# A decoder layer with routed experts on one core: block lists of six fixed experts from ranks alone, the shift added as rows are turned, the left-over branch between blocks 25 and 26, final sums of two tiles on TensorE

## The chip, the cores and the metric

The kernel runs on one core of one Trainium2 chip. The metric is the device time of one execution in microseconds (us). The core has a matrix engine (TensorE, "PE" in the profile, its weight loads "PEld"), a vector engine (DVE), a scalar engine (ACT), GpSimd (POOL), and SyncE (SP), which here only issues DMA transfers. Each engine works through its own instructions in order and waits on semaphores for the others. Transfers issued by SP and ACT go through hardware queues, those with a list of row numbers (gathers and scatters) are issued by POOL.

## The reference

One step of a hybrid decoder layer for 512 prompt rows and 8 sample rows, all in float32. The first part (projection, sparse attention, a convolution branch, output projection, residual) is untouched by the change. What follows it matters here:

```python
# x: residual rows (512 prompt rows + 8 sample rows, D = 1024); mods: 6 adaLN vectors
h = rmsnorm(x, norm2_g) * (1.0 + mods[4]) + mods[3]     # scale, then shift
# group = top-1 of 4, experts = top-2 of its 8; w: their two weights
y = sum over the 2 chosen experts e of
        w_e * (silu(h @ w_gate[e]) * (h @ w_up[e])) @ w_down[e]   # 1024 -> 256 -> 1024
x = x + mods[5] * y
y_out = rmsnorm(x, final_g)
```

There are 32 experts. A row goes to two of them; the numbers are known only once the router has run.

## The kernel before

The rows of all experts are put in blocks of 64 places. There are 36 ordinary blocks: the six experts with fixed places (their 18 weight tensors of 1 MiB are fetched ahead of the routing, `fetch`) have blocks 0 to 5, the four fullest of the others two blocks each, the rest one. 16 more blocks take what is left over; they stand in a branch (`tc.If(nxv > 0)`) that isn't taken with these data.

**Routing.** For each tile of 128 rows `project` forms the residual `x1`, `rows` scales it by its inverse root (ACT), by `A2b` (POOL, L1280), adds the shift `B2b` (POOL, L1281) and writes the rows `h` to `hrow` in memory. `choose` picks the experts on DVE, `place` turns ranks into places. Once the last tile (3) is ranked, DVE forms the block lists: which row stands in each place (`gix`), where its result goes (`six`), its weight (`wtb`), and which expert follows which (`exi`, by which SP addresses the weights of blocks 6 and on).

**Expert stage.** A pair of blocks is handled together: `gather` (POOL, L1627) fetches the 128 rows of a pair from `hrow` by `gix`, `turned` transposes them on PE (L1640, eight 128x128 pieces in two halves) and copies the halves out, one on ACT and one on DVE. For each block `up` multiplies by gate and up weights (L1650, gate and up products side by side), `hidden` forms silu times up on ACT and DVE, `flip` transposes that (L1663), `down` multiplies by the third weight (L1672), DVE scales the result (`ot`, L1676) and POOL scatters it into `yrow` (L1677). `run` sets the order: the down product of a block comes after the up product of the next; gather(p+1) is issued when pair p is turned. The weights come through SP, three loads of 1 MiB per expert, into 21 pages that are handed out again in the order in which they come free; eight loads can be outstanding.

**Branch.** After block 35 each engine loads `nxi` and compares (L1730, L1731). On the path not taken POOL does one more step, an ISA instruction that the profile calls INC_SWDGE_SEM: it brings the counters of POOL's eight transfer queues to where the branch would have left them.

**Final stage.** The scattered results are loaded as four tiles (`yt`, two halves of 512 KB each), added to the residual on DVE (L1754, L1758), squared on ACT, rooted on POOL, scaled on DVE (L1777) and stored. The sample rows (`ysq`, `fs`) are summed on POOL (L1781 to L1783).

A scheduler orders instructions on each engine by the order of the code and by `issue_after`, which pins an instruction behind another.

Of the kernel before, what the change touches and what calls it, by code (L numbers as in the profile page):

```python
# [24 lines left out]
NF = 6  # L25
# [6 lines left out]
GT, TH, TF = (), (1, 1, 1, 2), (1, 1, 1, 2)  # L32
# [148 lines left out]
def body(tc, I, O, dbg=lambda *a: None):  # L181
# [658 lines left out]
    A2T, B2T = cp.tile([128, 8], F32, name="A2T"), small("B2T")  # L840
# [242 lines left out]
    x1s = cp.tile([128, 256], F32, name="x1s", tag="c2")  # L1083
    zs = e2.tile([128, 4, 32], F32, name="zs", bufs=1)
# [75 lines left out]
    BO = box(3, 10, NBLK, half_=True)  # L1160
    OH3 = BO.rearrange("p f a b -> p (f a b)")[:, :960].rearrange("p (a b c) -> p a b c", a=10, b=3)
# [17 lines left out]
    def choose(i):  # L1179
# [17 lines left out]
        V.tensor_tensor(Cb[:, i], OH[:, i, 0], OH[:, i, 1], op=ALU.add)  # L1197
        pps[i] = tps("pps", (128, 32))
# [4 lines left out]

    def place(i):
        m = eb
        V.tensor_tensor(m, OH[:, i], pps[i].unsqueeze(1).to_broadcast([128, 2, 32]), op=ALU.mult)
        r, k, r_ = rk[:, 0, 2 * i:2 * i + 2], kk[:, 2 * i:2 * i + 2], rk[:, 1, 2 * i:2 * i + 2]
        V.tensor_reduce(r, m, axis=AX.X, op=ALU.add)
# [3 lines left out]
        for j in range(2):  # L1212
# [6 lines left out]
                        s3.unsqueeze(3).to_broadcast([128, 2, 3, 32]), op=ALU.mult)  # L1219
        V.scalar_tensor_tensor(k, k, -1.0, s3[:, :, 2], op0=ALU.mult, op1=ALU.mult)  # L1220
        if i == 4:
            V.tensor_scalar(k, k, K("inv"), None, op0=ALU.add)

    def new_rows():
# [8 lines left out]
        V.tensor_tensor(h2s, h2s, m4[:, 3], op=ALU.add)  # L1233
        for q in range(4):
            S.dma_start(hrow[512:520, :].rearrange("b (c r j) -> b c r j", r=4, j=32)[:, :, q],
                        h2s[32 * q:32 * q + 8].rearrange("p (c j) -> p c j", c=8))
# [13 lines left out]
    def project(i, n):  # L1250
# [5 lines left out]
        V.scalar_tensor_tensor(xh, pA, ra[:, 0, i:i + 1], xh, op0=ALU.mult, op1=ALU.add)  # L1256
        SP.dma_start(xrow[128 * i:128 * i + 128, 512 * n:512 * n + 512], xh)
# [14 lines left out]
    def rows(i):  # L1272
# [12 lines left out]
        place(i)  # L1285
# [38 lines left out]
    later = []  # L1324
# [3 lines left out]
    def tile_start(i):  # L1328
# [15 lines left out]
        if i == WOI:  # L1344
            load_wo(0, 2)
            for v, r in ((A2b, 4), (B2b, 3)):
                SP.dma_start(v, mrow[r - 2:r - 1, :].to_broadcast([128, 1024]))
# [129 lines left out]
    fetch(PRE[2])  # L1477

    pct = tps("pct", (32, 1))
    pcb = acc("pcb", (128, 32))  # L1480
    for n, i in enumerate(order):
        PE.matmul(pct, Cb[:, i, :], onb[:, 0:1], start=(n == 0), stop=(n == 4))
    for n, i in enumerate(order):
        PE.matmul(pcb, onb, Cb[:, i, :], start=(n == 0), stop=(n == 4))
    hl = cp.tile([32, 12], BF16, name="hl")
    V.scalar_tensor_tensor(hl[:, 0:1], pct, 64.0, K("dmask")[:32], op0=ALU.is_gt, op1=ALU.mult)
    V.tensor_tensor(hl[:, 1:2], K("dmask")[:32], hl[:, 0:1], op=ALU.subtract)
    V.tensor_scalar(hl[:, 4:12], K("thr")[:32], pct, None, op0=ALU.is_lt)
    with nc.allow_low_precision(reason="a whole number up to 8"):
        V.tensor_reduce(hl[:, 2:3], hl[:, 4:12], axis=AX.X, op=ALU.add)  # L1490
    px = acc("px", (128, 3, 33))
    col = lambda k: hl[:, k:k + 1].to_broadcast([32, 128])
    PE.matmul(px[:, 0, :], col(0), K("su")[:32, :33], start=True, stop=True)
    PE.matmul(px[:, 1, :], col(1), K("su")[:32, :33], start=True, stop=False)
    PE.matmul(px[:, 1, :], col(0), K("al")[:32, :33], start=False, stop=True)
    PE.matmul(px[:, 2, :], col(2), K("su")[:32, :33], start=True, stop=True)

    T = cp.tile([128, 3, 32], BF16, name="T")
    hB = cp.tile([128, 32], F32, name="hB")
    q = cp.tile([128, 4, 33], F32, name="q")  # L1500
# [12 lines left out]
    with tc.issue_after(mark["V"].ins):
        V.tensor_copy(pos[:, P_], K("eio")[:, :NF])
# [304 lines left out]
```

## Time and profile before

| | us |
|---|---|
| three runs of the kernel before | 792.86, 795.72, 796.38 (median 795.72) |
| the profiled execution | 789.56 |
| its span, first to last instruction | 787.8 |
| mean granted TensorE clock, share of full speed | 0.944 |
| PE busy | 683.7 (87% of the span) |
| DVE busy | 440.4 (56%) |
| ACT, POOL busy | 213.7 (27%), 208.3 (26%) |

A timeline row of the profile gives the start, the duration, the engine, the line, the operation with output and inputs and their shape, the number of instructions, and in brackets how long the engine stood idle before it and for whom it waited. L1650 is line 1650 of the kernel before. "q" behind an engine's name marks what its sequencer does, such as issuing a transfer. A window row gives busy time and, in brackets, the number of instructions of each engine within a stretch, then the granted clock (1.00 is 2.4 GHz, 0.50 is 1.2 GHz), the share of time that the 16 DMA engines were busy, and what they moved.

### The profile page before, as it was taken

Reading aid. Unit: us, or ns where it says so; the run is one execution under the profiler, and the core shown is the slowest. Engines: PE = TensorE matmul, PEld = TensorE weight load, DVE = VectorE, ACT = ScalarE, POOL = GpSimd, SP = SyncE. Lnnn points to the kernel's source line nnn. Section 1 sums busy time; section 2 is a strip of 40 time slices with the busy share of each in tenths; the row PEclk is TensorE's granted clock in tenths of the full one; section 3 lists DMA queues with packets and bytes.
Section 4 is the critical chain, followed back from the end, with each engine's and each line's share of the span. In section 5 each row is a group of like instructions: output and inputs, shape, how many; then the busy total and the mean of one; then the engine's idle time right before and its main releaser. Section 6 shows DMA issues by size and latency. Waiting matters only on the chain. (4 is left out here: it accounts for less than half of the span.)

```text
span 787.8 us, 12614 instructions
## 1 busy us (share of the span) xinstructions
PE 683.7 (87%) x4888; PEld 414.4 (53%) x4888; DVE 440.4 (56%) x960; ACT 213.7 (27%) x491; POOL 208.3 (26%) x182
## 2 busy tenths in 40 slices
PE   4999888997999988999789998289999999999910
PEld 3655777775786446644435444155555555554400
DVE  2444729999985758723776745843333333333245
ACT  1255721121113457634245323010110101010001
POOL 5134305035030101135602303312222222221114
PEclk9999999998999999999979999589999999999965
DMA  9985425644799303700004666679999999999954
GB/s 340 420 324 203 160 81 215 244 161 192 266 343 407 136 2 131 285 0 1 1 16 165 248 251 240 257 248 418 420 406 350 410 418 418 417 419 420 370 177 176
DMA packets 42332, 200.02 MB, mean 254 GB/s; under 512 B 10733, under 2 KB 14205, under 8 KB 22677
## 3 DMA queue, kind: packets, MB, share of 16 engines
q1 hardware_dynamic: 29341, 156.27, 50.7%
q0 software_dynamic: 10336, 40.95, 13.5%
q10 hardware_dynamic: 2592, 1.95, 0.8%
q8 instruction: 40, 0.66, 0.3%
q14 instruction: 23, 0.19, 0.1%
HBM read 187.82 MB, written 22.15 MB: 267 GB/s over the span
## 5 line engine op out<-in xcount | busy, mean ns | idle before, releaser
L591 DVE SCALAR_TENSOR_TENSOR y<-u,c,y 128x511 f32<-128x511 f32 (+23 forms) x120 | 103.7, 896 | 2.1
L1655 ACT ACTIVATE hd<-pgu 64x256 f32<-64x256 f32 x36 | 13.5, 375 | 200.4 <-PE pgu L1650 200.4
L1677 POOL DMA_INDIRECT yrow<-ot,six x36 | 39.1, 1085 | 99.4 <-DVE ot L1676 87.9
L1650 PE MATMUL pgu<-eu,mB 128*64 128x256 f32 x256 | 61.7, 384 | 1.9 <-DMA eu<-in_WU 1.9
L1650 PE MATMUL pgu<-eg,mB 128*64 128x256 f32 x256 | 62.2, 384 | 0.0
L1672 PE MATMUL pd<-ed,hTe 128*64 128x512 f32 x240 | 57.3, 598 | 0.8 <-issue 0.8
L1650 PE MATMUL pgu<-eu,mA 128*64 128x256 f32 x224 | 54.0, 384 | 1.8 <-DMA eu<-in_WU 1.8
L1650 PE MATMUL pgu<-eg,mA 128*64 128x256 f32 x224 | 54.2, 384 | 0.0
L1676 DVE SCALAR_TENSOR_TENSOR ot<-pd,wtb,mt 128x512 f32<-128x512 f32 x36 | 27.0, 751 | 44.3 <-PE pd L1672 44.3
L1656 DVE TENSOR_TENSOR hd<-pgu,hd 64x256 f32<-64x256 f32 x36 | 15.4, 428 | 59.1 <-ACT hd L1655 59.1
L1650 PEld LDWEIGHTS pgu<-eg,mB 128*64 128x64 f32 x256 | 32.8, 136 | 19.9 <-issue 5.1
L1381 ACT ACTIVATE P<-pSp,ast 128x128 f32<-128x128 f32 (+3 forms) x64 | 33.2, 534 | 24.2 <-DVE ast L1376 23.9
L1376 DVE TENSOR_REDUCE ast<-pSp 128x1 f32<-128x384 f32 (+3 forms) x44 | 27.3, 632 | 21.7 <-PE pSp L1371 21.6
L1650 PEld LDWEIGHTS pgu<-eg,mA 128*64 128x64 f32 x224 | 28.9, 136 | 17.3 <-issue 4.6
L225 DVE COPY hTe<-hTp 128x128 f32<-128x128 f32 x36 | 10.5, 291 | 48.3 <-PE hTp L1663 48.3
L370 PE MATMUL pr<-cTs,wc 128*64 128x256 f32 x256 | 37.1, 400 | 0.0
L1253 PE MATMUL woA<-wo,qT 128*128 128x512 f32 x64 | 35.9, 681 | 0.2 <-DVE rt L1175 0.2
L1650 PEld LDWEIGHTS pgu<-eu,mB 128*64 128x64 f32 x256 | 33.0, 136 | 4.0 <-DMA eu<-in_WU 2.8
L361 PE MATMUL cT<-CI,cR 128*128 128x128 f32 x128 | 21.1, 302 | 10.9 <-DVE cR L386 10.7
L1650 PEld LDWEIGHTS pgu<-eu,mA 128*64 128x64 f32 x224 | 28.9, 136 | 2.9 <-DMA eu<-in_WU 2.3
L1109 PE MATMUL woC<-wo,y 128*128 128x512 f32 x64 | 30.2, 605 | 0.1
L1413 PE MATMUL oT<-P,kv 128*64 128x512 f32 x80 | 28.6, 614 | 0.0
(572 smaller groups left out, 1654.5 us busy)
## 6 DMA issues: line engine op xcount, KB each, us to landing
eg<-in_WG SPq DMA_DIRECT2D x26, 1024.0 KB
eu<-in_WU SPq DMA_DIRECT2D x26, 1024.0 KB
ed<-in_WD SPq DMA_DIRECT2D x26, 1024.0 KB
wada<-in_WA SPq DMA_DIRECT2D x16, 1024.0 KB
wada<-in_WA POOLq DMA_DIRECT2D x8, 1024.0 KB, 15.2
WG<-in_WG SPq DMA_DIRECT2D x6, 1024.0 KB
WU<-in_WU SPq DMA_DIRECT2D x6, 1024.0 KB
WD<-in_WD SPq DMA_DIRECT2D x6, 1024.0 KB
```

Of the source, the lines that this page charges most:

```text
L361: PE.transpose(p[:, j, :], R[b:b + n, c, k, 2 * s8:2 * s8 + 2, :], ident[b:b + n, b:b + n])
L370: mark["PE"] = PE.matmul(self.pr[r][64 * c:64 * c + 64], wc1[:, c, 8 * r + 4 * h + s, :], self.T[h][:, c, s], start=(h == 0 and s == 0), s ...
L591: V.scalar_tensor_tensor(yb[:, s_:CVS], ub[:, :CVS - s_], w(k), yb[:, s_:CVS], op0=ALU.mult, op1=ALU.add)
L1109: PE.matmul(p, zc[:, g, 128 * i:128 * i + 128], wo[2 * n + 1][:, g], start=(g == 0), stop=(g == 3))
L1253: PE.matmul(pA, oTp[:, g, 128 * i:128 * i + 128], wo[2 * n][:, g], start=(g == 0), stop=(g == 3))
L1376: V.tensor_reduce(st[k][:, 0, h0:h0 + nh], pS[k][:, :nh * L].rearrange("p (h l) -> p h l", h=nh), axis=AX.X, op=ALU.max, negate=True)
L1381: S.activation(P[k][:, g, :L], pS[k][:, o:o + L], AF.Exp, bias=st[k][:, 0, g:g + 1], accum_out=st[k][:, 1, g:g + 1])
L1413: PE.matmul(oT[64 * k:64 * k + 64, :].rearrange("p (g t) -> p g t", g=4), kv12[:, br - 1, kt, 128 + 64 * k:192 + 64 * k], P[k][:, :, 128 * ...
L1650: chain[0] = PE.matmul(pgus[b][64 * h:64 * h + 64, :], xT[:, c, 64 * s_:64 * s_ + 64], w[:, c, :], start=(c == 0), stop=(c == 7))
L1672: chain[0] = PE.matmul(pd[64 * h:64 * h + 64, :], hT_[:, c, :], wd[:, c, 512 * h:512 * h + 512], start=(c == 0), stop=(c == 1))
L1676: V.scalar_tensor_tensor(ot, pd, wtb[:, b:b + 1], mt, op0=ALU.mult, op1=ALU.mult)
L1677: st = G.indirect_dma_start(out=yrow[:, :], out_offset=bass.IndirectOffsetOnAxis(ap=six[:, b:b + 1], axis=0), in_=ot, in_offset=None, boun ...
```

## The change

Four edits are made together.

1. **Lists of the six fixed experts from ranks alone.** Their blocks are known before the order of the other experts is. `static_part` and `static_rows` form the first three columns of `gix` from ranks, and gather(0) and gather(1) are issued there. The turning and the up products of blocks 0 and 1 are written in between the rest of the routing; `exi` moves ahead of them, and turned(1,0) stands behind `wtb`. `place(3)` comes after the turning of pair 0.
2. **The shift is added when rows are turned.** `hrow` holds rows without the shift. POOL's multiplication by `A2b` is done in halves before the inverse root, ACT scales in place, POOL's addition is gone. `turned` adds the shift (`B2c`, one value for each of the 1024 columns) while it copies the transposed rows out, both halves on DVE.
3. **The left-over branch stands after block 25** (`LEFT = 26`), the run of ordinary blocks being split in two; four spare pages instead of nine; gather(13) is repeated inside the branch.
4. **Final stage.** The sums of tiles 0 and 2 (`TP`) are made on PE by products with the identity into PSUM; everything goes by halves of 512 columns; `yt` is loaded as four 1 MiB transfers, the sample rows through ACT's queue; the sample rows are summed on DVE, the roots of tiles 2 and 3 come from ACT and DVE, and the order is written out.

```diff
+LEFT, TP = 26, (0, 2)
     def project(i, n):
+        (V if i + n == 4 else G).tensor_tensor(h2b[i % 2][:, 512 * n:512 * n + 512], xh, A2b[:, 512 * n:512 * n + 512], op=ALU.mult)
     def rows(i):
-        hop = S.activation(h2, x1[i], AF.Copy, scale=rs2[:, i:i + 1])
-        G.tensor_tensor(h2, h2, A2b, op=ALU.mult)
-        G.tensor_tensor(h2, h2, B2b, op=ALU.add)
+        S.activation(h2, h2, AF.Copy, scale=rs2[:, i:i + 1])
         SP.dma_start(hrow[128 * i:128 * i + 128, :], h2)
         choose(i)
-        place(i)
+        if i < 3:
+            place(i)
+    def static_rows():
+        RsF = small("RsF").bitcast(BF16).rearrange("p (j s) -> p j s", j=4)
+        rank(3)
+        for j in range(2):
+            V.tensor_scalar(RsF[:, j], K("slot"), rk[:, 0, 6 + j:7 + j], None, op0=ALU.is_equal)
+        pf = acc("pf", (128, NF))
+        for n, i in enumerate(order):
+            for j in range(2):
+                for f in range(2):
+                    chain[0] = PE.matmul(pf, RsF[:, j] if i == 3 else Rs[:, i, j], BS[:, f, 2 * i + j],
+                                         start=(n + j + f == 0), stop=(n == 4 and j + f == 2))
+        gf = pf.rearrange("p (a s) -> p a s", s=2)
+        for s_ in range(2):
+            op = V.tensor_scalar(gix[64 * s_:64 * s_ + 64, 0:NF // 2], gf[64 * s_:64 * s_ + 64, :, s_], BIG, None, op0=ALU.add)
+    gi = static_rows()
+    gather(0)
+    gather(1)
...
+    turned(0, 0, op)
+    turned(0, 1, mark["V"])
+    up(0, at(ahead[0]), range(8))
+    place(3)
...
+        op = hidden(0)
+    up(1, at(ahead[1]), range(0, UP))
+    flip(0)
+    up(1, at(ahead[1]), range(UP, 8))
...
+    op = V.tensor_copy(wtb, pb[:, 2])
+    turned(1, 0, op)
+    hidden(1)
-    run(todo, asked)
+    run(todo[:LEFT], asked)
+    sg, su = page("sg"), page("su")
+    spare = [[sg, su, page(f"sd{j}")] for j in range(2)]
+    nxv = nc.values_load(nxi[0:1, 0:1])
+    with tc.If(nxv > 0):
+        chain[0] = None
+        gather(OV0 // 2)
+        run([(b, lambda b=b: left(b - OV0)) for b in range(OV0, NBLK)], asked)
+        gather(LEFT // 2)
+    chain[0] = None
+    run(todo[LEFT:], asked)
...
     def total(i, hs=(0, 1)):
+            if i in TP:
+                with in_turn():
+                    PE.matmul(py[i][h], ident, t0[:, c], start=False, stop=False)
+                    chain[0] = PE.matmul(py[i][h], ident, t1[:, c], start=False, stop=True)
+                z = py[i][h]
```

POOL's instructions around the path not taken, first of the kernel before (the branch's last transfers of the path taken, then the ISA step, then the final stage; `DMASW` are POOL's transfer queues):

```order
L1677 DMA yrow<-ot,six 2080x512 [waits DMASW6_49,DVE_49]
L1622 DMA sd_6383<-in_WD,xix 128x2048 [waits DMASW7_49,PE_49]
L1677 DMA yrow<-ot,six 2080x512 [waits DMASW0_49,DVE_49]
L1677 DMA yrow<-ot,six 2080x512 [waits DMASW1_49,DVE_49]
L1731 UNCONDITIONAL_BRANCH
L1731 ISA [waits DMASW4_49,DMASW5_49,DMASW3_49,DMASW6_49,DMASW2_49,DMASW7_49,DMASW1_49,DMASW0_49]
L1731 UNCONDITIONAL_BRANCH
```

and of the changed kernel, where the same three rows are followed by the gathers and scatters of blocks 26 to 35:

```order
L1600 DMA yrow<-ot,six 2080x512 [waits DMASW3_49,DVE_49]
L1600 DMA yrow<-ot,six 2080x512 [waits DVE_49]
L1793 UNCONDITIONAL_BRANCH
L1793 ISA [waits DMASW4_49,DMASW5_49,DMASW3_49,DMASW6_49,DMASW2_49,DMASW7_49,DMASW1_49,DMASW0_49]
L1793 UNCONDITIONAL_BRANCH
L1548 DMA mA<-hrow,gix 128x1024 [waits DMASW5_49,DMASW4_49,PE_49]
L1548 DMA mB<-hrow,gix 128x1024 [waits DMASW6_49,PE_49]
L1548 DMA mA<-hrow,gix 128x1024 [waits DMASW7_49,DMASW5_49,PE_49]
L1600 DMA yrow<-ot,six 2080x512 [waits DMASW0_49,DVE_49]
```

What stood behind the ISA step were the roots and sample sums of the final stage; now the ordinary gathers 14 to 16 and ten scatters do.

PE between blocks 25 and 26 of the kernel before (`mB` holds the rows of gather(13), the products `pd` are the down product of block 24, those of `pgu` the up product of block 26):

```order
L1640 MATMUL xTp<-CI,mB 128x128 [waits DMASW5_49,PE_49]
L1640 MATMUL xTp<-CI,mB 128x128 x3
L1672 MATMUL pd<-ed_5748,hTe 64x512 [waits DMAHW7_49,DVE_49]
L1672 MATMUL pd<-ed_5748,hTe 64x512 x3
L1640 MATMUL xTp<-CI,mB 128x128 [waits PE_49]
L1640 MATMUL xTp<-CI,mB 128x128 x3
L1650 MATMUL pgu<-eg_5851,mB 64x256 [waits DMAHW3_49,Activation_49]
L1650 MATMUL pgu<-eu_5852,mB 64x256 [waits DMAHW4_49]
```

of the changed kernel, up to the branch (the down products of blocks 24 and 25 with the flip of block 25 between them):

```order
L1595 MATMUL pd<-ed_5795,hTe 64x512 [waits DMAHW2_49,DVE_49]
L1595 MATMUL pd<-ed_5795,hTe 64x512 x3
L1586 MATMUL hTp<-CI,hd 128x64 [waits DVE_49]
L1586 MATMUL hTp<-CI,hd 128x64
L1595 MATMUL pd<-ed_5840,hTe 64x512 [waits DMAHW5_49,DVE_49,Activation_49]
L1595 MATMUL pd<-ed_5840,hTe 64x512 x3
L1792 TENSOR_LOAD nxi [waits DVE_49]
L1793 COMPARE_AND_BRANCH
```

and behind the branch:

```order
L1793 UNCONDITIONAL_BRANCH [waits PE_49]
L1561 MATMUL xTp<-CI,mB 128x128 [waits DMASW5_49,DMASW6_49,DVE_49,PE_49]
L1561 MATMUL xTp<-CI,mB 128x128 x3
L1561 MATMUL xTp<-CI,mB 128x128 [waits DVE_49,PE_49]
L1561 MATMUL xTp<-CI,mB 128x128 x3
L1573 MATMUL pgu<-eg_6754,mB 64x256 [waits DMAHW6_49,DVE_49]
L1573 MATMUL pgu<-eu_6755,mB 64x256 [waits DMAHW7_49]
```

The turning of pair 13 stood around the down product of block 24; now it stands behind the branch, after both down products, and waits on two of POOL's queues.

DVE at the end of the lists of the kernel before, from the last step of the block matrix to the weights (`hl`, `q`, `T` and `ov`, formed further ahead, order the experts):

```order
L1529 TENSOR_TENSOR rt<-RC,rt 128x520
L1531 TENSOR_TENSOR rt<-rt,RC 128x520
L1541 TENSOR_SCALAR gix<-ptb 64x26 x2
L1546 TENSOR_TENSOR eb<-pos,CI 32x32
L1562 TENSOR_TENSOR rt<-rt 128x5x4
L1565 TENSOR_TENSOR rt<-rt 128x5
L1547 TENSOR_REDUCE rt<-eb 32x1
```

and of the changed kernel from the ranks of tile 3 to the first lists:

```order
L1212 TENSOR_TENSOR eb<-rt,pps 128x64
L1213 TENSOR_REDUCE rt<-eb 128x2
L1241 TENSOR_SCALAR RsF<-RC,rt 128x128 x2
L1250 TENSOR_SCALAR gix<-pf 64x3 x2
L1650 SCALAR_TENSOR_TENSOR hl<-pct,RC 32x1
L1652 TENSOR_SCALAR hl<-RC,pct 32x8
```

and further on, from `exi` over the turned rows of pair 0 (L1563) to the last step of place(3):

```order
L1699 CAST exi<-pex 1x26
L1563 TENSOR_TENSOR mA<-xTp,B2c 128x512 x2
L1219 TENSOR_TENSOR rt<-rt,RC 128x16
L1220 TENSOR_REDUCE rt<-rt 128x2
L1221 SCALAR_TENSOR_TENSOR rt<-rt 128x2
L1225 TENSOR_SCALAR rt<-rt 128x2
L1226 TENSOR_SCALAR rt<-rt 128x2
L1223 TENSOR_SCALAR rt<-RC,rt 128x128 x2
L1227 TENSOR_SCALAR rt<-rt 128x2
L1228 TENSOR_TENSOR rt<-rt 128x192
L1232 SCALAR_TENSOR_TENSOR rt<-rt 128x2
```

The list for the first gather now stands before the steps that order the experts, and place(3) with the block matrix stands behind the two halves of the turned rows of pair 0.

## Rows read from the trace of the kernel before

**Rows 1.** Windows: the whole span, then routing and expert stage.

```profile
core 0 of [0], span 787.8 us
...
500.00:520.00 20.00, 8.21 (x88) 6.30 (x89) 16.03 (x73) 2.92 (x5) 3.11 (x3) 0.53 0.61 221
...
660.00:700.00 40.00, 40.00 (x294) 20.86 (x291) 14.78 (x30) 4.04 (x9) 9.84 (x9) 1.00 1.02 417
```

**Rows 2.** Timeline of the routing of tile 3, DVE, POOL and PE.

```profile
493.97 1.52 DVE L1184 SCALAR_TENSOR_TENSOR rt<-rt,rs,bw 128x36 f32<-128x36 f32 x1
495.52 2.34 POOL L1281 TENSOR_TENSOR mB<-mB 128x1024 f32<-128x1024 f32 x1
...
495.72 2.16 DVE L1174 SCALAR_TENSOR_TENSOR eq<-rt,RC 128x4 f32<-128x4 f32 x1
...
498.81 0.25 DVE L1174 SCALAR_TENSOR_TENSOR eq<-le,rt,RC 128x32 f32<-128x32 f32 x1
...
501.05 0.19 PE L1202 MATMUL pps<-rt,RC 128*128 128x32 bf16 x1 [6.90 <-DVE rt L1197]
```

**Rows 3.** Timeline from the lists to the first two pairs of blocks.

```profile
509.79 0.38 DVE L1541 TENSOR_SCALAR gix<-ptb 64x26 int32<-64x26 f32 x2 [1.14 <-PE ptb L1535]
...
510.45 1.12 POOL L1627 DMA_INDIRECT mA<-hrow,gix  x1 [12.60 <-DVE eb L1546]
...
515.95 1.95 PE L1640 MATMUL xTp<-CI,mA 128*128 128x128 f32 x8
516.17 0.21 DVE L1580 COPY wtb<-ptb 128x52 f32<-128x52 f32 x1
...
517.83 0.69 PE L1650 MATMUL pgu<-WG,mA 128*64 128x256 f32 x1
...
525.83 0.66 PE L1640 MATMUL xTp<-CI,mB 128*128 128x128 f32 x4
```

**Rows 4.** Landing of the 18 gathers of line L1627.

```profile
DMA to landing us min/median/max: 3.4/8.6/10.0
```

**Rows 5.** Waits of 515 to 752: engine, line, releaser: us, times, longest.

```profile
PEld pgu L1650 <- DMA eu<-in_WU: 5.1, 3, 2.3
```

**Rows 6.** Timeline of the expert stage, block 24 and the last two blocks.

```profile
673.84 0.75 DVE L1676 SCALAR_TENSOR_TENSOR ot<-pd,wtb,mt 128x512 f32<-128x512 f32 x1 [0.86 <-PE pd L1672]
...
677.59 0.66 PE L1640 MATMUL xTp<-CI,mB 128*128 128x128 f32 x4
...
680.83 0.68 DVE L225 COPY mB<-xTp 128x512 f32<-128x512 f32 x1
...
746.49 1.89 PE L1672 MATMUL pd<-ed,hTe 128*64 128x512 f32 x8
...
749.47 1.94 PE L1672 MATMUL pd<-ed,hTe 128*64 128x512 f32 x8 [0.83 <-issue]
...
752.48 0.98 POOL L1677 DMA_INDIRECT yrow<-ot,six  x1 [1.79 <-DVE ot L1676]
```

**Rows 7.** Landing of scatters (L1677): all 36, then the nine of 665–722.

```profile
DMA to landing us min/median/max: 2.6/7.2/10.1
...
DMA to landing us min/median/max: 6.6/8.0/9.2
```

**Rows 8.** Instructions of the branch's line: ns min/median/max, first and last start.

```profile
L1731 POOLq EVENT_SEMAPHORE  x4: 17/42/43, 755.5 to 755.7; - x4
...
L1731 PEldq COMPARE_BRANCH  x1: 3987/3987/3987, 750.1 to 750.1; - x1
...
L1731 POOLq INC_SWDGE_SEM  x1: 1996/1996/1996, 755.8 to 755.8; - x1
```

**Rows 9.** Timeline of the final stage, SP and DVE.

```profile
757.77 1.75 SPq L1745 DMA_DIRECT2D yt<-yrow  x4
...
761.93 1.23 DVE L1754 TENSOR_TENSOR xt<-xt,yt 128x1024 f32<-128x1024 f32 x1 [3.36 <-DMA yt<-yrow]
...
771.97 1.74 DVE L1777 SCALAR_TENSOR_TENSOR yt<-yt,rsf,gf 128x1024 f32<-128x1024 f32 x1
```

More of the change, by code (lines that the diff above doesn't have):

```diff
@@ L1589, in body @@
[L1589 to L1597 removed]
+    fetch(3 * NF - sum(PRE[:2]) - sum(FI))
     xg, xTs = [A2b, B2b], h2b
@@ L1691, in run @@
             W = W()
[L1692 removed]
+            if n == 0 and b:
                 turned(b // 2, 0)
                 turned(b // 2, 1)
[L1695 to L1701 removed]
+            if b > 1:
+                up(b, W, range(0, UP))
+                if before:
+                    flip(before[0])
+                up(b, W, range(UP, 8))
+                if b % 2 and n + 1 < len(blocks):
+                    turned(b // 2 + 1, 0)
+                hidden(b)
             if before:
@@ L1708, in run @@
         down(*before)
-    pgus, hds, hTs_, scat = {}, {}, {}, []
-    chain = [lastw]
-    asked = {0, OV0 // 2, NBLK // 2}
+    pgus, hds, hTs_, scat, silu = {}, {}, {}, [], [None]
+    asked = {0, 1, OV0 // 2, NBLK // 2}
+    gi = static_rows()
     gather(0)
-    fetch(3 * NF - sum(PRE) - sum(FI))
+    gather(1)
+    rest = ExitStack()
+    rest.enter_context(tc.issue_after(gi.ins))
+    pct = tps("pct", (32, 1))
+    pcb = acc("pcb", (128, 32))
+    for n, i in enumerate(order):
+        PE.matmul(pct, Cb[:, i, :], onb[:, 0:1], start=(n == 0), stop=(n == 4))
@@ new lines, in body @@
+    up(1, at(ahead[1]), range(0, UP))
+    flip(0)
+    up(1, at(ahead[1]), range(UP, 8))
+    rest = ExitStack()
+    rest.enter_context(tc.issue_after(mark["V"].ins))
+    pb = acc("ptb", (128, 3, NBLK))
+    rest.enter_context(tc.issue_after(chain[0].ins))
+    for f in (1, 2):
+        for a in range(10):
+            chain[0] = PE.matmul(pb[:, 0, :], Rs[:, a // 2, a % 2], BO[:, f, a], start=(f == 1 and a == 0), stop=(f == 2 and a == 9))
+    six = cp.tile([128, NBLK], I32, name="six")
+    wtb = cp.tile([128, NBLK], F32, name="wtb")
@@ new lines, in body @@
+    ge = pb[:, 0].rearrange("p (a s) -> p a s", s=2)
+    for s_ in range(2):
+        V.tensor_scalar(gix[64 * s_:64 * s_ + 64, NF // 2:], ge[64 * s_:64 * s_ + 64, NF // 2:, s_], BIG, None, op0=ALU.add)
+    for a in range(5):
+        PE.matmul(pb[:, 1, :], Rs[:, a, 1], BO[:, 0, 2 * a + 1], start=(a == 0), stop=(a == 4))
+    t6 = small("t6", NBLK)
+    V.tensor_scalar(t6, pb[:, 1], 2.0, K("half"), op0=ALU.mult, op1=ALU.add)
+    V.scalar_tensor_tensor(six, pb[:, 0], 4.0, t6, op0=ALU.mult, op1=ALU.add)
@@ L1728, in body @@
         SP.dma_start(half(xt[i // 2], i % 2), xrow[128 * i:128 * i + 128])
-    spare = [[page(f"sg{j}"), page(f"su{j}"), page(f"sd{j}")] for j in range(3)]
-    nxv = nc.values_load(nxi[0:1, 0:1])
-    with tc.If(nxv > 0):
-        chain[0] = None
-        gather(OV0 // 2)
-        run([(b, lambda b=b: left(b - OV0)) for b in range(OV0, NBLK)], asked)
     ry = yrow.rearrange("(t a) f -> t (a f)", a=4)
@@ L1796, in body @@
+    root(2)
+    total(3, (1,))
+    final(2)
+    root(3)
+    final(3)
     es.close()
```

399 lines of the change are left out of this document (217 added, 182 removed).

## The prediction

> **What bounds the kernel now.** I read the windows by stage first. In 660–700 PE is busy 40.00 of 40 us at full clock while the DMA share is 1.02 [rows 1]: the expert stage keeps PE and the queues full together, so a microsecond taken out of its middle by PE is a microsecond of the span, and an engine other than PE matters there only if PE waits for it. In 500–520 the same row reads PE 8.21 of 20 us at a granted clock of 0.53: this is the routing stage, a chain of short DVE steps that ends in the lists, a gather, and the first products. The reader should see three waits, since the change moves all of them. The first is the way from the last ranks (501.05) over the lists (509.79) and the first gather (510.45) to the first gate product (517.83) [rows 2, 3]. The second stands at the end of the expert stage, where PE waits 5.1 us in all for weights [rows 5]. The third follows the last scatter: issued at 752.48, while the first load of the final stage goes out at 757.77, the moment that INC_SWDGE_SEM of 1996 ns from 755.8 ends [rows 6, 8, 9].
>
> The sum is made in the frame of the profiled execution (span 787.8 us [rows 1], run 789.56) and added to the median of 795.72: the profiled run is 6.2 us faster than that median, and I have no row that says where those 6.2 us lie, so only the difference is carried over. About 0.5% (4.0 us) is what a measurement of this kernel can tell from no change.
>
> **The shift out of the rows: part of the lead-in.** POOL's two 128x1024 steps after the inverse root go away or move ahead of it. Under them DVE is slow: the same L1174 takes 2.16 us on 128x4 while POOL's step of 2.34 us runs, and 0.25 us on the larger 128x32 once POOL is idle; L1184 before it takes 1.52 us [rows 2]. About 1.9 us and, taking 0.5 us for the second (between 0.25 and 1.52, near the other small steps), 1.0 us come back on DVE; with 0.4 us for the same at tile 2 the last ranks come at about 497.7 instead of 501.05, 3.3 us earlier. The shift is now added by DVE where ACT or DVE copied the turned rows. That is 17 more DVE steps of the size of `ot` (0.75 us) against copies of 0.68 us [rows 6], and the second copy of a pair already ends just as PE wants it. At 0.07 us for each half that PE waits on, 17 pairs give 1.2 us; half of the pairs may hide it. I take **+0.6 us**, between 0 and 2.5.
>
> **The lists of the six fixed experts.** From ranks alone, two DVE steps, 20 short matmuls and the two gix steps (0.38 us [rows 3]) are left, about 2.2 us: gather(0) goes out at about 500 instead of 510.45. Landing took 3.4 to 10.0 us [rows 4]; I take 6, as weights are being fetched at that time: 506. The eight transposes at 1.95 us and the products behind them (1.88 us after the first transpose [rows 3]) put the first product at about 508 instead of 517.83. Ten microseconds are not gained, however, because PE runs out of lists: the next pair of blocks is turned only after `wtb`, by the order shown above. From the last ranks to wtb it takes 501.05 to 516.17, 15.1 us [rows 2, 3]. Starting at 497.7 that ends at 512.9, but DVE now does the static lists (1.5 us), two turned halves (1.5 us), a hidden product and a copy (0.7 us) inside that chain. It stands still for about 2 us until the gather has landed (nothing behind the turned halves can overtake them), and the list products wait behind the products of blocks 0 and 1 on PE, about 3 us: 521.6 to 522. The transposes of pair 1 stood at 525.83 [rows 3]: 3.8 us earlier. Some of that is lost again, as PE then still has block 0's down product to do and restarts after a gap. I take **−2.5 us**, between 0 (the inserted work eats all) and −5.5 (gather at 3.4 us, no wait on PE).
>
> **The left-over branch amid the stage.** This is the largest term. In the trace the branch stands at the end; not taken, it costs a jump on each engine, and on POOL an INC_SWDGE_SEM that waits until every indirect transfer has landed. Whoever waits on one of those queues after it waits for POOL: the load at 757.77 starts when that step ends, though it needs only the scatter, which had landed at 752.48 + 2.6 = 755.1 [rows 6 to 9]. After the change, PE's first transposes behind the branch wait on two of those queues. So PE's loss is counted along this chain. After the gate and up products of block 25 end (677.59) PE does down(24), flip and down(25), which took 4.92 us at the end of the stage (746.49 to 749.47 + 1.94) [rows 6]: 682.5, of which 0.7 us is idle. The scatter starts 1.07 us after that (752.48 against 751.41), lands 8.0 us later, the median in that part of the stage (6.6 to 9.2 [rows 7]), POOL needs 0.7 us to come to its increment (755.1 to 755.8) and 2.0 us for it [rows 8]: PE waits 11.8 us. Its own jump (3987 ns [rows 8]) lies beside that. Then the transposes run at the half clock, 1.95 us for eight [rows 3] against 1.3 for two fours of 0.66 [rows 6], and the next products at 0.69 instead of 0.38 for about four pairs, together +1.0. Sum 0.7 + 11.8 + 1.0 = **+13.5 us**; with landings of 6.6 and 9.2 it is 12.1 to 14.7.
>
> What it gives back: DMA goes on meanwhile, since eight 1 MiB loads are outstanding (8 x 2.5 us at 417 GB/s [rows 1], 20 us) and weights for blocks 26 to 30 are asked for before the branch. PE's waits for weights at the end, 5.1 us [rows 5], should go, as PE is 11 us later there and the loads aren't: **−5.1 us**. And the final stage no longer stands behind POOL's increment: 757.77 − 755.1 = **−2.7 us** [rows 8, 9]. Four spare pages in place of nine cost nothing while the branch isn't taken, but four loads after it wait for the increment; I hide that under those 20 us.
>
> **The final stage.** From the first load (757.77) DVE starts at 761.93 and works almost without a break; steps of 1.23 us become 1.74 while POOL works [rows 9]. The change takes two tiles' additions (four steps of 1.23 us for each pair) to PE and the sample's steps from POOL to DVE. DVE's work falls from about 19 to 16.3 us, but its first step now waits for sample rows that come late (some 6 us after the first load instead of 4.2), PE adds at the half clock, and each root of tiles 2 and 3 is five short steps over two engines. I take **+0.5 us**, between −1.5 and +3.
>
> **Sum:** −2.5 + 0.6 + 13.5 − 5.1 − 2.7 + 0.5 = **+4.3 us**: span 792.1, time 800.0.
>
> **The rivals.** (A) PE isn't held by POOL's increment at the branch, but by its own jump: 0.5 + 4.0 us [rows 8] in place of 11.8. PE's loss is 6.2 us, the sum −3.0 us, 792.7. For it speaks that PE needs only rows of a gather that landed long before; against it the load at 757.77, which was held in just this way. (B) The lead-in gives its full 5.5 us and DVE's relief in the final stage is felt (−1.5): 4.3 − 3.0 − 2.0 = −0.7 us, 795.0. For it speaks that 9.5 us of lateness of the first product are taken away; against it, that wtb still ends the chain. (C) On the slow side: what passes the branch goes through full queues. The scatters in the quiet end are among the fast ones (2.6 us against 8.0 [rows 7]); if the instructions behind the jump are slowed like that, by 8.0/2.6 from 4.0 us to some 12 us, POOL comes to its increment 3 us later, and gather(14), issued only behind it, lands at 10.0 [rows 4] instead of just in time, 1 us more: +8.3 us, 804.0. It decides as soon as such a fetch takes longer than the 8.0 us landing that hides it. The Trainium skill ("Runtime: NRT & Kernel Launch", Instruction fetch mechanics) says that a taken branch whose target is outside the fetched window waits for a DMA fetch of the target. By that rule every engine pays at the branch, and (C) would hold if the fetch shares the queues' load; the trace agrees only for PE (3987 ns), and no run here shows such a jump under full queues. (D) The change doesn't move the wait but splits the stage's loads: SP stands at the loads behind the increment until the queues run dry, and the 5.1 us stay: +9.4 us, 805.1. Against it are the 20 us outstanding.
>
> **How the numbers follow.** Forecast 0.45 (of it slower 0.28, same 0.17, since it ends at the bound), A 0.15 (same 0.07, faster 0.08, with a lead-in better than 2.5), B 0.18 (same 0.13, faster 0.05), C 0.12 and D 0.05 (slower), and 0.05 for a final stage far better than counted (faster). Faster 0.18, same 0.37, slower 0.45. The range takes in A with a lead-in of −5.5 (789.7) and C with a final stage of +3 (806.5): 790 to 807.
>
> **What would show it.** Right: a PE gap of about 12 us near 680–692 at a granted clock that falls to 0.5, its end on POOL's INC_SWDGE_SEM; no DMA waits of PE afterwards; the first product near 508 and the products of block 2 near 526; the first final load right after the last scatter's landing. Wrong: PE's gap under 7 us (A), first transposes of pair 1 before 520 (B), a compare-and-branch longer than 8 us on PE or POOL (C), PE waits for weights after 700 (D).

## The result and the profile after

The changed kernel is a little slower: 799.42 us (median of 17 runs, 795.95 to 807.40) against 794.64 us (17 runs of the kernel before, 788.82 to 796.96). The medians differ by 4.8 us, the means by 6.3; the ratio, which lies near that of the means, is 1.008, interval 1.0058 to 1.0101, which is 6.4 us (4.6 to 8.0). Forecast were 800.0 us and +4.3 us: the time lies 0.6 us from the forecast, while the difference is 0.5 us larger by the medians and some 2 us larger by the ratio. That the time fits better than the ratio is luck: the median of before over 17 runs lies 1.1 us under the 795.72 that the sum was added to.

The profiled execution of after took 798.0 us, span 795.9, mean clock 0.954. Both kernels are timed here from the first product of `woC`, the last work ahead of the edits (334.22 in before, 335.72 in after). That start lies between 334.2 and 340.9 in the fourteen profiles of this study, also among kernels that read alike up to it, so absolute times of two profiles don't compare. The stretches below come from one profile each.

| from the first `woC` product | before | after | forecast | measured |
|---|---|---|---|---|
| last ranks | 166.8 | 163.3 | −3.3 | −3.5 |
| first gather issued | 176.2 | 165.9 | about −10.5 | −10.4 |
| first gate product | 183.6 | 174.8 | about −9.8 | −8.8 |
| `wtb` | 182.0 | 189.7 | +5.4 to +5.8 | +7.8 |
| transposes of pair 1 | 191.6 | 189.5 | −3.8 | −2.1 |
| down(24) | 344.0 | 342.1 | −1.9 (−2.5 + 0.6) | −1.9 |
| down(24) to first final load | 79.6 | 84.9 | +5.7 (13.5 − 5.1 − 2.7) | +5.3 |
| first final load to the end | 30.0 | 33.2 | +0.5 | +3.1 |
| end of the span | 453.6 | 460.2 | +4.3 | +6.6 |

The routing, from the timeline of after (start, duration, engine, line, operation, count, idle time before it):

```profile
335.72 0.68 PE L1112 MATMUL woC<-wo,y 128*128 128x512 f32 x1
...
499.01 0.19 PE L1209 MATMUL pps<-rt,RC 128*128 128x32 bf16 x1 [3.22 <-DVE rt L1202]
501.58 1.10 POOL L1548 DMA_INDIRECT mA<-hrow,gix  x1 [8.53 <-DVE hB L1670]
508.63 1.94 PE L1561 MATMUL xTp<-CI,mA 128*128 128x128 f32 x8 [4.75 <-DMA mA<-hrow,gix]
509.76 0.69 DVE L1563 TENSOR_TENSOR mA<-xTp,B2c 128x512 f32<-128x512 f32 x1 [5.66 <-PE xTp L1561]
510.50 0.69 PE L1573 MATMUL pgu<-WG,mA 128*64 128x256 f32 x1
...
519.52 0.69 PE L1726 MATMUL ptb<-rt 128*128 128x52 bf16 x20
...
525.23 1.10 PE L1561 MATMUL xTp<-CI,mB 128*128 128x128 f32 x4
525.44 0.21 DVE L1759 COPY wtb<-ptb 128x52 f32<-128x52 f32 x1 [0.68 <-PE ptb L1758]
```

Against [rows 2] and [rows 3] the gather goes out 2.6 us after the last ranks instead of 9.4, and the gate products follow it. But DVE stands 5.66 us until the gather has landed and been turned, with the rest of the lists behind it. The block matrix is ready at 516.9, and the list products (L1726) come 2.6 us later, at 519.52, behind the products of blocks 0 and 1. `wtb` now comes as late as the transposes of pair 1, where PE has run dry. The windows of after show that, and the hole at the branch (PE, PEld, DVE, ACT, POOL busy, clock, DMA share, GB/s):

```profile
500.00:520.00 20.00, 12.54 (x102) 8.01 (x103) 10.65 (x49) 3.67 (x6) 3.10 (x3) 0.66 0.62 233
520.00:525.00 5.00, 1.70 (x39) 1.34 (x35) 4.33 (x18) 0.69 (x2) 0.00 (x0) 0.89 0.98 347
...
676.00:700.00 24.00, 12.80 (x78) 6.90 (x76) 4.80 (x9) 0.38 (x1) 4.70 (x5) 0.79 1.01 414
```

In [rows 1] PE had 8.21 us of 500–520; here it has 12.54, then 1.70 of the next five. At the branch it has 12.80 of 24 us, while the DMA share stays at 1.01. The timeline there:

```profile
677.83 1.89 PE L1595 MATMUL pd<-ed,hTe 128*64 128x512 f32 x8
680.81 1.94 PE L1595 MATMUL pd<-ed,hTe 128*64 128x512 f32 x8 [0.83 <-issue]
683.82 1.05 POOL L1600 DMA_INDIRECT yrow<-ot,six  x1 [1.79 <-DVE ot L1599]
693.12 1.94 PE L1561 MATMUL xTp<-CI,mB 128*128 128x128 f32 x8 [10.37 <-DMA yrow<-ot,six]
693.95 1.04 POOL L1548 DMA_INDIRECT mA<-hrow,gix  x1 [9.08 <-DMA yrow<-ot,six]
```

and the instructions of the branch's line (ns min/median/max, first and last start):

```profile
L1793 POOLq EVENT_SEMAPHORE  x4: 17/43/1492, 689.5 to 691.2; - x4
L1793 PEldq COMPARE_BRANCH  x1: 6163/6163/6163, 681.4 to 681.4; - x1
L1793 DVEq COMPARE_BRANCH  x1: 72/72/72, 683.5 to 683.5; - x1
L1793 POOLq INC_SWDGE_SEM  x1: 1716/1716/1716, 691.3 to 691.3; - x1
```

PE stops at 682.75 and goes on 10.37 us later. Its own jump is over at 681.4 + 6.2 = 687.6. POOL's semaphore step of 1492 ns ends at 691.10, just as the trace's record of that semaphore has the last piece of the scatter of 683.82 landing (691.07). POOL's increment ends at 691.3 + 1.7 = 693.0, and PE, POOL's gather and the work behind them start within a microsecond. The transfers of after in the time of PE's jump, 681.4 to 687.7, have instruction packets among them (queue, kind: packets, MB, share of the 16 DMA engines' time):

```profile
q8 instruction: 1, 0.02, 1.0%
q14 instruction: 2, 0.02, 0.7%
```

Rows like [rows 5] are gone: the profile of after has no wait of PE for weights behind the routing. The final stage of after:

```profile
760.40 0.98 POOL L1600 DMA_INDIRECT yrow<-ot,six  x1 [1.79 <-DVE ot L1599]
...
762.74 2.15 SPq L1825 DMA_DIRECT2D yt<-yrow  x4
762.75 3.30 ACTq L1821 DMA_DIRECT2D ysq<-yrow  x4
...
768.02 2.08 PE L1865 MATMUL py<-yt,CI 128*128 128x512 f32 x2 [5.05 <-DMA yt<-yrow]
...
776.43 0.42 DVE L1836 TENSOR_TENSOR fs<-ysq 128x256 f32<-128x256 f32 x1 [16.31 <-DMA ysq<-yrow]
```

The first load follows the last scatter by 2.3 us instead of 5.3 ([rows 6, 9]). DVE, however, begins with the sample rows, and they come 13.7 us after the first load; in [rows 9] it began 4.2 us after it. PE had its first tile at 768.02.

### The profile page after: what moved, and what is told of

It is laid out like the page before. It is cut to its first block, busy times and chain, and to the rows that moved or that the text cites. A ratio compares the mean times of both kernels' runs of the same rounds, so it can differ in the third digit from the quotient of the medians.

```text
span 795.9 us, 12740 instructions
## 1 busy us (share of the span) xinstructions
PE 702.3 (88%) x4932; PEld 421.6 (53%) x4932; DVE 450.6 (57%) x1008; ACT 208.5 (26%) x485; POOL 192.8 (24%) x178
## 4 chain that ended last, share of the span: by engine, by line
PE 51%; DVE 18%; issue 15%; DMA 8%; POOL 4%; ACT 3%; ACTq 0%; POOLq 0%; DVEq 0%
DVE y L591 9%; PE pgu L1573 6%; PE pr L370 5%; DMA yrow<-ot,six 4%; PE woC L1112 3%; PE oT L1455 3%; PE pq L805 3%; PE woA L1292 3%; POOL yrow L1600 3%; PE cT L361 3%; PE pS L957 3%; PE pTp L1445 2%; PE pd L1595 2%; PE pkv L727 2%; PE pT L967 2%
## 5 line engine op out<-in xcount | busy, mean ns | idle before, releaser
L1578 ACT ACTIVATE hd<-pgu 64x256 f32<-64x256 f32 x36 | 13.5, 376 | 241.8 <-PE pgu L1573 241.8
L1573 PEld LDWEIGHTS pgu<-eg,mB 128*64 128x64 f32 x256 | 33.8, 139 | 21.5 <-issue 6.5
L1423 ACT ACTIVATE P<-pSp,ast 128x128 f32<-128x128 f32 (+3 forms) x64 | 33.3, 535 | 16.9 <-DVE ast L1418 16.7
L225 DVE COPY hTe<-hTp 128x128 f32<-128x128 f32 x36 | 10.5, 291 | 41.7 <-PE hTp L1586 39.7
L1573 PEld LDWEIGHTS pgu<-eu,mB 128*64 128x64 f32 x256 | 33.8, 139 | 0.0
L1292 PE MATMUL woA<-wo,qT 128*128 128x512 f32 x64 | 33.6, 639 | 0.2 <-DVE x1a L1295 0.2
```

The source lines that it names most:

```text
L1292: PE.matmul(pA, oTp[:, g, 128 * i:128 * i + 128], wo[2 * n][:, g], start=(g == 0), stop=(g == 3))
L1423: S.activation(P[k][:, g, :L], pS[k][:, o:o + L], AF.Exp, bias=st[k][:, 0, g:g + 1], accum_out=st[k][:, 1, g:g + 1])
L1573: chain[0] = PE.matmul(pgus[b][64 * h:64 * h + 64, :], xT[:, c, 64 * s_:64 * s_ + 64], w[:, c, :], start=(c == 0), stop=(c == 7))
```

## The experiments

Each was timed beside the kernel before on the same chip (e1 to e4 on one, e5 to e8 on a second, e9 to e12 on a third; 6 runs of e1 and e4, 12 of the others). The table collects them; the stretches are those of the table above, and the first column says on which kernel each was made. In e8 the first final load is that of the sample rows.

| run | ratio to before (interval) | down(24) after first `woC` | to first final load | final stage |
|---|---|---|---|---|
| before | 1 | 344.0 | 79.6 | 30.0 |
| after | 1.0080 (1.0058 to 1.0101) | 342.1 | 84.9 | 33.2 |
| e5, before + branch at 26 | 1.0035 (1.0005 to 1.0065) | 343.8 | 84.3 | 30.5 |
| e1, after, branch at the end | 1.0110 (1.0076 to 1.0143) | 345.2 | 80.7 | 35.7 |
| e6, the same, other table load | 1.0046 (1.0012 to 1.0080) | 345.2 | 80.6 | 34.0 |
| e2, after, no branch | 1.0038 (1.0014 to 1.0062) | 345.3 | 77.2 | 33.8 |
| e3, after, sample rows later | 1.0053 (1.0026 to 1.0080) | 344.6 | 83.9 | 30.5 |
| e8, after, sample rows ahead on SP | 1.0056 (1.0021 to 1.0091) | 344.9 | 84.1 | 30.7 |
| e4, after, lists first | 1.0119 (1.0081 to 1.0156) | 345.5 | 84.0 | 33.5 |
| e7, after, more of the lists ahead | 1.0037 (1.0003 to 1.0071) | 339.9 | 84.7 | 33.3 |
| e9, after, `B2b` loaded | 1.0076 (1.0048 to 1.0104) | 342.0 | 85.0 | 33.0 |
| e10, before + shift edit | 0.9956 (0.9930 to 0.9981) | 341.1 | 79.2 | 30.2 |
| e12, e10 with `B2b` loaded | 0.9932 (0.9898 to 0.9965) | 339.8 | 79.2 | 32.1 |
| e11, after + e3 + e7 + e9 | 1.0002 (0.9974 to 1.0031) | 338.1 | 85.5 | 31.1 |

**The branch alone in the kernel before (e5).**

```diff
-    run(todo, asked)
+    run(todo[:26], asked)
+    ...  # four spare pages, the branch, gather(13) inside it
+    run(todo[26:], asked)
```

> The kernel before with only the third edit: the left-over branch between blocks 25 and 26, four spare pages. Theory (PE loses 12 to 13 us at the branch, 5 us of its waits for weights go, the first final load no longer stands behind POOL's increment): the time from the down product of block 24 to the first final load grows from 79.6 us by 4 to 5 us, and the kernel is 4 to 5 us slower than before. Rival (the edit moves the branch at no net cost, since the kernel with all other edits and the branch at the end was no faster than the changed one): within 1.5 us of the kernel before.

Timeline of e5:

```profile
693.29 1.94 PE L1640 MATMUL xTp<-CI,mB 128*128 128x128 f32 x8 [10.27 <-DMA yrow<-ot,six]
```

The hole is 10.3 us in a kernel that has none of the other edits, and the stretch around it is 4.7 us longer; the waits for weights are gone here too. The whole is 2.8 us slower (0.4 to 5.2; the medians differ by 1.1). So the branch's cost and its two returns are shown for the stretch; that the whole pays all 4.7 us is inside the interval but not proved by it.

**The branch at the end of the changed kernel (e1, e6), and none (e2).** The first two move the block behind block 35, the third drops it (the path for left-over rows is then missing).

```diff
-    run(todo[:LEFT], asked)
-    ...  # spare pages, branch
-    run(todo[LEFT:], asked)
+    run(todo, asked)
```

> The changed kernel with the left-over branch back behind block 35. Theory (the branch amid the stage costs PE about 12.9 us, gives back 5.2 us of waits for weights and 2.9 us at the first final load): 4.8 us faster than the changed kernel, so 0 to +3 us against the kernel before; PE waits for weights near the end of the stage come back (4 to 6 us), and no PE gap near 683 to 693. Rival (the loss lies in the routing, in the shift on DVE or in the final stage): still 4 us or more slower than before.

> The changed kernel without the branch: the path for left-over rows, which isn't taken with these data, is left out. Theory: as with the branch at the end, but without its 2 us increment on POOL and its jump in front of the final stage, so some 2.5 to 3 us faster than that kernel and -3 to 0 us against the kernel before. Rival (the increment is hidden in the landing of the last scatter): the same time as with the branch at the end.

> The changed kernel with the branch behind block 35 as before, but with the square root's table loaded behind the branch, so that the two table loads of 1.3 us inside the final stage of the first such kernel are gone. Theory: the final stage is 33 us instead of 35.7, the whole 2.5 us faster than that kernel, and 3 to 4 us from the down product of block 24 to the first final load are saved against the changed kernel. Rival (the branch costs the same at either place): the time of the changed kernel.

e1 gave the 4 us back in its stretch and lost 2.5 in the final stage: the step that readies ACT's square root stood ahead of the branch, and ACT loaded its tables twice behind it, 1.28 us each, at 778.5 and 788.4. That is a flaw of e1, not of the change, and its whole is no faster; e6 has that step behind the branch and reads 1.0046 against 1.0080, with intervals that overlap. Its waits (engine, line, releaser: us, times, longest):

```profile
PEld pgu L1573 <- DMA eu<-in_WU: 5.8, 4, 2.3
PE pgu L1573 <- DMA eu<-in_WU: 3.9, 3, 1.9
```

With the branch away from the middle the waits for weights return, as in [rows 5], and the stretch falls from 84.9 to 80.6. e2, which has those waits too (5.6 us), shows what the branch costs at either place: its stretch is 7.7 us shorter than that of after, 2.4 us shorter than that of before and 3.4 shorter than that of e6. At the old place the price is mostly POOL's increment ahead of the first final load (forecast 2.7): that load goes out 5.5 us after the last scatter's issue in e6 and 2.3 in e2.

**The sample rows (e3, e8).** e3 puts their sums behind final(0), with final(1) next; e8 issues their loads on SP's queue, ahead of the tiles.

```diff
-    sample()
     total(0)
     total(1)
-    sample_root()
...
     final(0)
+    sample()
+    sample_root()
+    final(1)
...
-    final(1)
```

```diff
-        S.dma_start(ysq[32 * q:32 * q + 8]...
+        SP.dma_start(ysq[32 * q:32 * q + 8]...
```

> The changed kernel with the sample rows summed on DVE behind the sums and the first store of tile 0 and 1 instead of first. Theory (DVE stands 16 us for the sample rows, which land 11 us after their last issue, and 3.1 us of the final stage's length come from that): 3 us faster than the changed kernel (2 to 5). Rival (PE's sums at the half clock and the roots set the final stage): within 1 us of the changed kernel.

> The changed kernel with the four loads of the sample rows issued through SP ahead of the four 1 MiB loads, instead of through ACT's queue beside them. Theory (the sample rows' many short pieces share the DMA engines with 4 MiB of long ones and so land 11 us after their last issue): they land 4 to 6 us after it, DVE's first final step comes 6 to 8 us after the first load instead of 13.7, the tiles' loads 2.7 us later, and the final stage is 3 us shorter than 33.2. Rival (the landing is slow by the number of pieces alone): 11 us again, and the final stage 1 to 3 us longer.

Timeline of e3:

```profile
775.38 2.75 DVE L1836 TENSOR_TENSOR xt<-xt,yt 128x512 f32<-128x512 f32 x4 [10.69 <-DMA yt<-yrow]
```

and of e8:

```profile
769.85 2.89 SPq L1821 DMA_DIRECT2D ysq<-yrow  x4
774.51 0.43 DVE L1836 TENSOR_TENSOR fs<-ysq 128x256 f32<-128x256 f32 x1 [7.37 <-DMA ysq<-yrow]
```

In after the sample rows reach DVE 10.4 us after their last issue (776.43 − 766.05); in e8, with the same pieces ahead of the tiles on the tiles' own queue, 1.8 us (774.51 − 772.74). Both kernels take 2.5 to 2.7 us out of the final stage, nearly all that it had grown by. So the growth is DVE's wait for small transfers that lie beside 4 MiB of tiles; the additions on PE and the roots are as in after and leave little of it to explain. One profile's final stage isn't sharper than about 2 us, however: e12, whose final stage is that of before, has 32.1 against 30.0 to 30.5 in before, e5 and e10. The groups still stand apart (six kernels with edit 4 as in after or e6: 33.0 to 34.0; e3, e8 and e11: 30.5 to 31.1). Neither moves the whole by more than the intervals leave open (1.0053 and 1.0056 against 1.0080).

**The lists (e4, e7).** e4 puts place(3) and the block matrix ahead of the turning on DVE, and the 20 list products that `gix` needs ahead of block 1 on PE. e7 takes the five products for `six` there as well, puts flip(0) behind `wtb`, and so no longer holds DVE's list steps behind that flip. The products for `wtb` itself stay behind block 1 in both.

```diff
-    turned(0, 0, op)
-    turned(0, 1, mark["V"])
-    up(0, at(ahead[0]), range(8))
     place(3)
...
+    turned(0, 0, op)
+    turned(0, 1, mark["V"])
+    up(0, at(ahead[0]), range(8))
+    # the list products (e4: the 20 for gix; e7: also the 5 for six)
```

> The changed kernel with the ranks of tile 3 and the block matrix on DVE ahead of the turned rows of pair 0, and the list products on PE ahead of the products of block 1. Theory (the lead-in gained nothing because DVE stood 5.7 us for the gather and the list products stood behind blocks 0 and 1): products of block 2 near 524 instead of 529, and 4 us faster than the changed kernel (2 to 5). Rival (weights bind from there, or the lists are held by ACT's table loads): less than 1 us.

> The changed kernel with tile 3's ranks and the block matrix ahead of the turned rows of pair 0 on DVE, all list products ahead of block 1's products on PE, and the flip of block 0 behind the weights wtb. Theory (in the first such kernel the wait only moved: two list products still stood behind block 1 and the DVE list steps behind the flip of block 0): wtb 32 us after the last output-projection product instead of 34.9, products of block 2 some 3 us earlier, 3 us faster than the changed kernel. Rival (weights bind from there on): less than 1 us.

e4 gained nothing: the products for `six` and DVE's list steps were still behind block 1 and the flip of block 0, and `wtb` came 191.6 us after the first `woC` product, against 190.7 to 190.8 in e1 to e3. The wait had only moved. Timeline of e7, whose first `woC` product is at 338.75:

```profile
526.47 0.21 DVE L1758 COPY wtb<-ptb 128x52 f32<-128x52 f32 x1 [0.51 <-PE ptb L1757]
526.63 0.66 PE L1561 MATMUL xTp<-CI,mB 128*128 128x128 f32 x4
```

`wtb` comes at 187.7, block 2 begins at 190.9 instead of 195.9 to 196.2 in e6 and e8 of the same chip, and down(24) at 339.9 instead of 344.9 to 345.2 (342.1 in after's own profile). So the order of the lists holds 2 to 5 us of the lead-in; which of e7's moves brings it, on PE or on DVE, these two runs don't part. The whole shows 1.0037 against 1.0080, intervals that just overlap.

**The shift alone (e10, e12), and `B2b` by its load (e9).** In the changed kernel POOL sets `B2b` to zero (L1386), where before loaded it. e10 makes edit 2 alone in the kernel before, with that step; e12 does the same but loads `B2b`; e9 loads it in the changed kernel.

```diff
# e9, in the changed kernel; e12 differs from e10 by the same line
-            G.memset(B2b, 0.0)
+            SP.dma_start(B2b, mrow[1:2, :].to_broadcast([128, 1024]))
```

> The kernel before with only the second edit: no shift in the rows, added when they are turned, with the POOL memset. Theory: first woC to first woA product 65.4 to 66.6 us instead of 63.7; first woA product to the last ranks 100 us instead of 103 (DVE no longer slowed under POOL); the lists and the first product 3 us earlier after the last woA product; as weights bind at the end of the expert stage, most of it is waited away there, and the kernel is within 2 us of the kernel before. Rival (what DVE gains in the routing reaches the end): 2 to 3 us faster than before.

> The changed kernel with one line undone: the buffer B2b is filled by its old load, not by a POOL memset (its contents reach no output). With the memset the scheduler put the woC products of one tile behind attention steps in another order on PE, DVE and ACT. Theory (this reordering, which no step of the prediction counted, costs time ahead of the routing): from the first woC to the first woA product 63.7 us as in the kernel before, instead of 65.4 to 66.6, and the kernel 2 us faster than the changed one (1 to 3). Rival (the later start of the routing in the changed kernels is scatter of the runs): that stretch stays at 65.4 or more, no difference.

> The kernel before with the second edit and B2b filled by its old load instead of the POOL memset, so that the order ahead of the routing stays as it was. Theory (the shift alone brings the weights of block 6 on 5 us earlier, and the memset's reordering takes 2 to 3 us of that away): first woC to first woA product 63.7 us instead of 66.5, 2 us faster than the second edit alone, 4 to 6 us faster than the kernel before. Rival (the stretch is shorter but the end isn't, as in the changed kernel with this one line undone): the time of the second edit alone, 3 us faster than before.

Timeline of e10:

```profile
334.40 1.96 PE L1112 MATMUL woC<-wo,y 128*128 128x512 f32 x4
...
498.05 0.18 PE L1205 MATMUL pps<-rt,RC 128*128 128x32 bf16 x1 [3.85 <-DVE rt L1200]
...
513.19 0.21 DVE L1587 COPY wtb<-ptb 128x52 f32<-128x52 f32 x1
513.28 0.35 SPq L1623 DMA_DIRECT2D eg<-in_WG  x1
```

Last ranks and `wtb` are both 3.2 us earlier than in before (163.7 and 178.8 after the first `woC` product), and the first weights of block 6 are asked for 0.1 us behind `wtb`, so they are 3.2 us earlier as well. The gain isn't eaten by the waits for weights at the end, which are 4.6 us instead of 5.1: down(24) comes 2.9 us earlier, and the whole is 3.5 us faster (1.5 to 5.6). With `B2b` loaded (e12) it is 5.4 us faster (2.8 to 8.1; medians 788.57 against 796.19 on the same chip): **faster than both kernels**, by less than 1%. Its profile, with the long final stage named above, ends only 2.5 us earlier than that of before, so the rest of the gain isn't located.

The POOL step takes 0.95 us, but with it the scheduler puts the attention and `woC` products in another order. Timeline of after:

```profile
349.89 2.74 PE L1112 MATMUL woC<-wo,y 128*128 128x512 f32 x6
```

and of e9:

```profile
334.50 3.68 PE L1112 MATMUL woC<-wo,y 128*128 128x512 f32 x8
...
345.50 2.74 PE L1112 MATMUL woC<-wo,y 128*128 128x512 f32 x6
```

The run of six that follows the first 16 products stands 11.0 us behind the first product in e9 and 14.2 us in after. From the first `woC` to the first `woA` product before, e5, e9 and e11 take 63.6 us, e12 64.2; the kernels with the step 65.4 to 66.7. Of the 1.8 us between after and e9, 0.2 are left at down(24), and the whole of e9 is as after (1.0076). Between e10 and e12 1.3 us are left there. So the reordering is shown; that it costs time at the end is not.

**All three mends (e11).** e3, e7 and e9 in one kernel.

> The changed kernel with three mends: list steps and list products ahead of block 1, sample rows summed late, B2b by its load. Theory (3.4 us before the branch, 2.7 us in the final stage and 2 us ahead of the routing add up): 7 to 8 us faster than the changed kernel, 2 to 3 us faster than the kernel before. Rival (weights bind, or the gains overlap): as fast as the kernel before or slower.

It is level with before (1.0002, 0.9974 to 1.0031) and about 6 us faster than the changed kernel; I had expected it ahead of before. Down(24) comes at 338.1, 5.8 us earlier than in before (343.96 against 338.14), and the branch's stretch takes 5.9 us of that back (85.5 against 79.6).

## Why the prediction was right, and where it was wrong

- **The branch: right, in mechanism and size.** PE's gap was forecast at 11.8 us behind 0.7 us of idle, and is 10.4 behind 0.8; it ends with POOL's increment. In the forecast's own terms: 1.07 us to the scatter's issue as forecast, 7.25 to its landing (forecast 8.0), 0.25 to the increment (0.7), 1.7 for it (2.0). What the gap was too long by, the half clock took: the granted clock falls within the gap and is 0.50 (1.2 GHz) from 693.1 to 698.0, where seven pairs of products start 0.42 us apart instead of 0.21 and the eight transposes take 1.9 us instead of 1.2; that is some 2 us, where 1.0 was forecast. That the loss of 13.5 us is met so closely (0.8 + 10.4 + 2) is in part two errors that cancel. The waits for weights went (−5.1 forecast; e6 and e2 have them back) and the first final load stands behind the scatter (−2.7 forecast; e2 −2.4 against before). The three together were +5.7 forecast, +5.3 in after, +4.7 in e5.
- **Rival A is dead:** PE's own jump ended 5.5 us before PE went on. **D too:** no waits for weights are left after 700.
- **Rival C was right in direction, but doesn't decide:** PE's jump rose from the 3987 ns of [rows 8] to 6163 ns with full queues, and POOL, too, came to its next step only 5.3 us behind its compare-and-branch (684.20 to 689.54) instead of 2.6 in before. It then still waited 1.5 us for the scatter, so the slower jump stayed hidden under the landing. The packet of 16 KB on q8 (an instruction packet, shown with the branch's rows above) starts 3.4 to 3.8 us after PE's compare-and-branch in the eight profiles with the branch amid the stage and 1.0 to 1.2 us after it in the five with it at the end; in all 13 PE's jump is over 1.4 to 1.5 us after that packet's end. Which engine a packet is for isn't named, but as far as the times show, the jump waits for this packet and is longer because it starts later. The Trainium skill ("Runtime: NRT & Kernel Launch", Instruction fetch mechanics) says that a taken branch whose target is outside the fetched window waits for a DMA fetch of the target. The trace agrees for PE and, by its late next step, for POOL, not for PE alone as the prediction read it; DVE went on 0.5 us behind its own compare-and-branch.
- **The lead-in: right in after, uncertain beyond it.** The steps fell nearly as forecast (table above), and the argument that `wtb`, not the gather, would end the chain held against B. But `wtb` came 2 us later than forecast. The term that was mis-sized is DVE's standstill for the gather, put at about 2 us and measured at 5.66; the wait of the list products behind blocks 0 and 1, put at about 3 us, was 2.6. The +0.6 for copies on DVE didn't show: from the transposes of pair 1 to down(24) e10, which has them, takes 152.4 us as before does. And five other kernels that read like after up to the branch (e1, e2, e3, e6, e8) had down(24) at 344.6 to 345.3: 0.6 to 1.3 us later than before, where after's one profile has 1.9 us earlier. The term lies between −1.9 and +1.3; forecast −1.9.
- **What the lead-in's sum hid.** It took the shift and the lists together and asked only when block 2 could start. Alone the shift brings 2.9 us at down(24) (e10): all that follows the last ranks comes some 3 us earlier. The lists from ranks then put `wtb` 10.9 us later (189.7 against 178.8) to have the gate products of block 0 5.7 us earlier. It isn't the weights that wait for `wtb` there: in after the first of block 6 are asked for at 515.75, 9.7 us ahead of it. By these profiles edit 1 as built is a loss at down(24) of 1.0 us in after against e10, of 2.2 in e9 against e12, and of more in the five kernels named above. Edits 1 and 4 were never run alone.
- **The final stage: wrong, the term mis-sized.** +0.5 was forecast with an upper bound of 3; it is +3.1. The failed step is "some 6 us after the first load" for the sample rows: it is 13.7 us. e3 and e8 remove 2.5 to 2.7 us by taking that wait away. In the profiles this makes up the forecast's shortfall of some 2 us.
- **Not counted:** the reordering ahead of the routing by POOL's new step.

The stretches of the two profiles add up to +6.6; the runs differ by 6.4 by the ratio (4.6 to 8.0) and by 4.8 by the medians. What stays open is the lead-in's share, which varies by 3 us between kernels that read alike up to there, and so the share of the branch in the whole (e5: 0.4 to 5.2).

## What to carry over

When a step waits for all queues of an engine, ask what stands behind it at its new place: at the end of the stage it held one load, amid the stage it holds PE. A first operand that is fetched sooner is worth nothing if the list that feeds all later work is put behind it; put that list first. And give an in-order engine its late, small operand last.

## What the runs showed of the hardware

- The jump over a branch's body cost PE 3624 to 4163 ns at the quiet end of the stage (five profiles; in before the DMA share is 0.16 in that time) and 6003 to 6263 ns amid it (eight; 1.02 in after). POOL came to its next step 2.6 to 2.8 us and 5.2 to 5.5 us behind its compare-and-branch. DVE's took 72 ns in both kernels.
- POOL's step on the path not taken took 1716 ns amid the stage and 1996 ns at its end; in after POOL first waited until its last scatter had landed, 7.25 us after the issue. PE and SP, which wait there on POOL's queues, went on only when that step had ended (693.12 and 692.99 in after).
- The sample rows, in pieces of 128 bytes, landed 10.4 us after their last issue on a queue of their own beside 4 MiB on the other, and 1.8 us after it ahead of them on the same queue. The Trainium skill ("DMA: Bandwidth & Descriptors", Queues, rings and completion order) says that a DMA engine takes turns between queues by whole packets. That a queue of small pieces gets little in each turn is my reading of it; the two runs go that way, though no row shows the turns.
- In e1 ACT loaded its tables twice behind the branch, 1.28 us each, although a step ahead of it had readied them (752.6); in e6, with that step behind the branch, one load is left there (768.9).
